# Moving the squares and the row statistics of the MLP norm into single slots of the tail's product loop

## The chip, the core and the metric

The kernel runs on one core of a Trainium2 chip. A core has a matrix engine (TensorE, PE in the profile, with its weight loads shown apart as PEld), a vector engine (VectorE, DVE), a scalar engine (ScalarE, ACT), GpSimd (POOL) and SyncE (SP), which here only issues DMAs. Matrix products are accumulated in PSUM, where eight banks of 128 x 512 float32 serve the stage in question; DVE and ACT read them out from there. The engines run side by side and wait for one another only through semaphores. The metric is the device time of one execution in microseconds (us), lower being better; the median over several runs is compared.

## The reference

A two-layer encoder trunk over 1024 positions and 1024 channels. Each layer is a mixer (layer 0: two recurrent head groups; layer 1: chunked attention), an output projection, an RMS-normed MLP with squared ReLU, and a gated embedding:

```python
x = x + mix
hf = rmsnorm(x, norm_ffn_g[i])
x = x + jnp.square(jax.nn.relu(hf @ mlp_w1[i])) @ mlp_w2[i]
x = x + rmsnorm(p[i] @ ple_w_proj[i], ple_norm_g[i]) * jax.nn.sigmoid(x @ ple_w_gate[i])
```

with `rmsnorm(x, g) = x * rsqrt(mean(x*x) + eps) * g`, the mean taken over the channels of one position. The change concerns only this mean for `hf`. ReLU and a positive factor for each position can be exchanged, so the kernel multiplies `x * g` by `w1` at once and brings in `rsqrt(...)`, squared, after the squared ReLU.

## The kernel before

Everything is held transposed: channels on the 128 partitions (eight tiles, `NK = 8`), positions along the free dimension (T = 1024, in two halves of `HB = 512`). Every float32 operand of a large product is split into a rounded part and a rest (`split`: one ACT copy, one DVE subtraction), and a product is three matrix instructions (`mm3`).

`tail(i, xsrc)` runs once for each layer, after the mixer. Its stages:

1. *Output projection.* For n = 0..7 the new residual is made: its first half lies in DRAM as `xh[n]`, the second half goes there as `xh2[n]` (tile name `xm`, line 1299).
2. *First MLP product*, in 16 units p = 0..15. A unit is a Strassen-like scheme of seven products m, run in `order = (1, 2, 5, 6, 7, 3, 4)`. One product is 12 matrix instructions into one bank of PSUM (`product`, line 1365). What follows it in the same iteration q of the inner loop is called its slot: sums and the squared ReLU on DVE and ACT (`plus`, `hidden`), and one of the seven weight pieces of the next unit (`prepare`). At a unit's start `raws(p + 1)` issues two 512 KB loads of weights on SP's queue into one of two tiles, `lt[2]` and `lt[3]`. For the first four units (`PLAIN = 4`) the hidden values are stored as they are; from the fifth on each is multiplied by `rs` (line 1384).
3. *Second MLP product*, then the *gate*.

The norm's statistics are made during stage 2. `squares(n)` (line 1309) loads the two halves of residual tile n (two DMAs of 256 KB on SP's queue, line 1314), squares them on ACT (line 1316, or 1319 for n = 0) and adds them on DVE into the two sums `accs` (line 1317). After unit p = 0, 1 and 2 come the squares 0 to 2, 3 to 5 and 6 to 7. Each takes a new tile with tag `pl`, of which there is one buffer, so that a square's loads wait for the addition of the square before. After unit 2 also come `row_stats` (line 366: eight products of the sums with a column of ones, fp32, which the trace shows as 16 matrix instructions, then 11 small DVE operations on 128 x 8 numbers for the inverse root, the result in `col`), `to_rows` (line 378: eight transposes with the identity, line 192, and two ACT copies out of PSUM) and one DVE product that squares `rs`.

Each engine executes its instructions in a fixed order. This order is made when the kernel is built, by a list scheduler that takes the program's order as priority and may put an instruction ahead of earlier ones that it reckons not to be ready; so loads, squares and weight pieces stand earlier in the trace than in the source. The fourth unit's products 5 and 6 stand ahead of the statistics in layer 0, but not in layer 1.

PSUM banks are taken in turn by `bank()` for products and statistics alike. `rs` is one tile of 128 x 1024 (tag `ph`), allocated before the loop and written by `to_rows` alone.

Of the kernel before, what the change touches and what calls it, by code (L numbers as in the profile page):

```python
# [8 lines left out]
F32 = mybir.dt.float32  # L9
# [3 lines left out]
ALU = mybir.AluOpType  # L13
# [4 lines left out]
P = 128  # L18
T = 1024
D = 1024  # L20
NK = D // P
HB = 512
# [87 lines left out]
class Trunk:  # L110
# [1091 lines left out]
    def tail(self, i, xsrc):  # L1202
# [9 lines left out]
        nc, tc, a = self.nc, self.tc, self.a  # L1212
        V, A, G = nc.vector, nc.scalar, nc.gpsimd
        last = i == 1
        hs = [slice(0, HB), slice(HB, T)]
        with ExitStack() as es:
# [16 lines left out]
            def ring(views):  # L1233
                state = [0]

                def f():
                    state[0] += 1
                    return views[(state[0] - 1) % len(views)]
                return f
            halves = lambda t: [t[:, q, :] for q in range(2)]  # L1240
            quarters = lambda t: [t[:, q, hs[e]] for q in range(2) for e in range(2)]
            two = lambda t: t.rearrange("p (q c) -> p q c", q=2)
            parts = lambda t: [two(v) for v in halves(t)]

            def tiles_x(dt):
                xw = [self.xp.tile([P, 3, T], dt, tag=f"xw{q}", name=f"xw{q}") for q in range(2)]
                return ([xw[k // 3][:, k % 3, :] for k in range(6)] +
                        [self.xp.tile([P, T], dt, tag=f"x{k}", name=f"x{k}") for k in (6, 7)])
# [11 lines left out]
            accs = [self.accp.tile([P, HB], F32, tag=f"acc{hf}", name="acc") for hf in range(2)]  # L1260
            col = self.cst.tile([P, NT], F32, tag="col", name="col")
# [4 lines left out]
            def split(c, s):  # L1266

                hi, lo = c[:, 0], c[:, 1]
                if len(s.shape) > 2:
                    hi, lo = (z.rearrange("p (j c) -> p j c", c=P) for z in (hi, lo))  # L1270
                A.copy(hi, s)  # L1271
                V.tensor_tensor(lo, s, hi.bitcast(F32), op=ALU.subtract)  # L1272
# [22 lines left out]
            def ev_out(n):  # L1295
# [10 lines left out]
                            split(cmb[m][j], u)  # L1306
                return f

            def squares(n):

                both = self.pre.tile([P, 2, HB], F32, tag="pl", name="xq")
                for hf, src in ((0, self.xh[n]), (1, self.xh2[n])):
                    t = both[:, hf]
                    nc.sync.dma_start(out=t, in_=src)
                    if n:
                        A.activation(t, t, AF.Square)
                        V.tensor_tensor(accs[hf], accs[hf], t, op=ALU.add)
                    else:
                        A.activation(accs[hf], t, AF.Square)
# [3 lines left out]
            def raws(p):  # L1323
                r = lt[3 - p % 2] if p else place(F32)
                for e in range(2):
                    nc.sync.dma_start(out=r[:, e], in_=a["w1"][i, 2 * p + e])
                prep[p] = [r[:, u].rearrange("p (j e c) -> p e j c", e=2, c=P)[:, v] for u in range(2) for v in range(2)], {}, []

            def prepare(p, m):

                (a11, a12, a21, a22), d, free = prep[p]
                if (p, m) == (0, 1):
                    d[m] = self.pre.tile([P, 2, HB], F32R, tag="pl", name="w1")
                else:
                    if not free:
                        free += parts(place(F32R))
                    d[m] = free.pop(0)
                if m == 5:

                    V.tensor_tensor(a21, a21, a22, op=ALU.add)  # L1340
                o, u, v = {1: (a11, None, None), 2: (a12, None, None), 5: (a21, None, None), 6: (a11, a21, a11),
                           4: (a22, None, None), 7: (a22, a22, a11), 3: (a12, a12, a11)}[m]
                if u is not None:
                    V.tensor_tensor(o, u, v, op=ALU.subtract)
                split(d[m], o)
# [14 lines left out]
            lt = lates([F32] * 4)  # L1360
            scr = ring([v for t in lt[0:2] for v in quarters(t)])
            rs = self.pre.tile([P, T], F32, tag="ph", name="rs")


            def product(p, m):
                ps, c = self.bank(), prep[p][1][m]
                for j in range(4):
                    o, z = slice(j * P, j * P + P), cmb[m][j]
                    self.mm3(ps, c[:, 0, o], c[:, 1, o], z[:, 0], z[:, 1], j == 0, j == 3)
                return ps  # L1370

            def plus(t, u, out=None):
                r = out if out is not None else scr()
                V.tensor_tensor(r, t, u, op=ALU.add)  # L1374
                return r

            def hidden(t, p, r, hf):

                A.activation(t, t, AF.Relu)  # L1379
                A.activation(t, t, AF.Square)  # L1380
                if p < PLAIN:
                    nc.scalar.dma_start(out=self.hd[2 * p + r][:, hs[hf]], in_=t)
                else:
                    V.tensor_tensor(t, t, rs[:, hs[hf]], op=ALU.mult)
                    if (r, hf) != (0, 1):
                        store(p, {(0, 0): 1, (1, 0): 2, (1, 1): 3}[r, hf], t)
                return t
# [4 lines left out]
            def differ(p, m, u, v, out=None):  # L1392
                t = out if out is not None else scr()
                V.tensor_tensor(t, u, v, op=ALU.subtract)
                store(p, m, t)
                return t
# [4 lines left out]
            def load_w2(g, u):  # L1401
                t, raw = place(F32R), self.pre.tile([P, 2, HB], F32, tag="pl", name="w2")
                for j in range(2):
                    nc.sync.dma_start(out=raw[:, j], in_=a["w2"][i, 2 * g + j, u])
                split(t, raw.rearrange("p j c -> p (j c)"))
                w2[g, u] = t[:, 0], t[:, 1]

            def fetch_hidden(g, k, t, raw):
                nc.sync.dma_start(out=raw, in_=self.hd[4 * g + k])
                return t, raw  # L1410

            def load_hidden(t, raw):
                V.tensor_tensor(raw, raw, rs, op=ALU.mult)
                split(t, raw)
# [32 lines left out]
                split(areas[m][q % 4], raw)  # L1447

            prep_order = (1, 2, 5, 6, 4, 7, 3)
            for m in prep_order[1:]:  # L1450
                prepare(0, m)
            for p in range(16):
                if p < 15:
                    raws(p + 1)
                else:
                    load_w2(0, 0)
                for q, m in enumerate(order):
                    ps = product(p, m)
                    if m == 1:
                        p1 = scr()  # L1460
                        A.copy(p1, ps)
                    elif m == 2:
                        c11 = hidden(plus(p1, ps), p, 0, 0)
                    elif m == 5:
                        p5 = ps
                    elif m == 6:
                        u2 = plus(p1, ps, p1)
                        u4 = plus(u2, p5)
                    elif m == 7:
                        u3 = plus(u2, ps, u2)  # L1470
                        c22 = hidden(plus(u3, p5), p, 1, 1)
                    elif m == 3:
                        c12 = hidden(plus(u4, ps, u4), p, 0, 1)
                        if p >= PLAIN:
                            differ(p, 7, c22, c12)
                            t1 = differ(p, 5, c12, c11, c12)
                            t2 = differ(p, 6, c22, t1)
                    else:
                        c21 = hidden(plus(u3, ps, u3), p, 1, 0)
                        if p >= PLAIN:  # L1480
                            differ(p, 4, c21, t2)
                    if p < 15:
                        prepare(p + 1, prep_order[q])
                    elif q == 1:
                        hid = [fetch_hidden(0, k, h0[k], lt[2 + k // 2][:, k % 2]) for k in range(4)]
                    elif 2 <= q < 6:
                        load_hidden(*hid[q - 2])
                    yield 0
                if p < 3:
                    for n in range(3 * p, min(3 * p + 3, NK)):  # L1490
                        squares(n)
                if p == 2:
                    self.row_stats(accs, col)
                    self.to_rows(col, rs)
                    V.tensor_tensor(rs, rs, rs, op=ALU.mult)
            x = tiles_x(F32)
            for k in range(NK):
                nc.sync.dma_start(out=x[k][:, hs[0]], in_=self.xh[k])
# [48 lines left out]
            for n in range(NB):  # L1547
                u, banks = n % 4, {}
                for s, m in enumerate(order2):
# [7 lines left out]
                    e, hf = goes[m]  # L1557
# [543 lines left out]
```

## Time and profile before

| what | value |
|---|---|
| median of 3 runs | 3112.31 us (3107.09 to 3116.35) |
| profiled execution | 3119.22 us, of which its span is 3117.5 us |
| mean granted clock of TensorE | 0.968 |
| layer 0, units of the first MLP product before the statistics | about 977 to 1042 us of the span |
| layer 1, the same | about 2388 to 2445 us of the span |
| statistics, layer 0 (first matrix instruction to the square of `rs`) | 1042.3 to 1051.6 us |
| statistics, layer 1 | 2445.1 to 2454.3 us |

The profile is taken from one execution. In its timeline a row is the start, the duration, the engine, the line, the operation, written tile `<-` read tiles, shapes and the number of instructions merged; in brackets the time for which the engine sat idle just before, and what ended that. Durations of matrix instructions overlap with their successors, so the pace of a run of them is read from the start of one row to the start of the next. In the windows view a row is a stretch: its length, then for PE, PEld, DVE, ACT and POOL the busy time and the count of instructions, then the granted clock of TensorE as a share of full speed, the busy share of the DMA engines and GB/s. In the view of waits a row tells who waited for whom: total, times, longest.

### The profile page before, as it was taken

Reading aid. Unit: us, or ns where it says so; the run is one execution under the profiler, and the core shown is the slowest. Engines: PE = TensorE matmul, PEld = TensorE weight load, DVE = VectorE, ACT = ScalarE, POOL = GpSimd, SP = SyncE. Lnnn points to the kernel's source line nnn. Section 1 sums busy time; section 2 is a strip of 40 time slices with the busy share of each in tenths; the row PEclk is TensorE's granted clock in tenths of the full one; section 3 lists DMA queues with packets and bytes.
Section 4 is the critical chain, followed back from the end, with each engine's and each line's share of the span. In section 5 each row is a group of like instructions: output and inputs, shape, how many; then the busy total and the mean of one; then the engine's idle time right before and its main releaser. Section 6 shows DMA issues by size and latency. Waiting matters only on the chain.

```text
span 3117.5 us, 47104 instructions
## 1 busy us (share of the span) xinstructions
PE 2998.6 (96%) x17288; PEld 2477.6 (79%) x17288; DVE 2222.7 (71%) x4518; ACT 1512.2 (49%) x2922; POOL 534.0 (17%) x978
## 2 busy tenths in 40 slices
PE   7999999999999999999999999999899999999999
PEld 5777777777777788888887988888788788888887
DVE  6646675667758788877866676776768688888862
ACT  4323433344436544544433577777766545444431
POOL 6524442443510000000005111110210000000002
PEclk8989999999999999999999999999999999999999
DMA  4212112212356444754424111110256444754433
GB/s 137 71 42 72 44 58 72 63 51 70 103 168 206 148 156 150 259 168 153 126 98 136 52 33 33 42 46 16 71 176 215 147 152 149 246 179 147 135 108 102
DMA packets 187639, 358.45 MB, mean 115 GB/s; under 512 B 45712, under 2 KB 47888, under 8 KB 187408
## 3 DMA queue, kind: packets, MB, share of 16 engines
q1 hardware_dynamic: 158608, 303.00, 30.0%
q10 hardware_dynamic: 28800, 52.44, 4.4%
q8 instruction: 136, 2.23, 0.3%
q14 instruction: 95, 0.78, 0.1%
HBM read 262.04 MB, written 93.32 MB: 114 GB/s over the span
## 4 chain that ended last, share of the span: by engine, by line
PE 81%; DVE 9%; ACT 4%; DMA 3%; issue 1%; POOL 1%; SPq 0%; DVEq 0%; POOLq 0%; ACTq 0%
PE dps L177 68%; PE ch L177 2%; PE po L177 2%; PE iz L177 1%; PE pm L177 1%; PE tp L177 1%; PE pt L192 1%; DVE ptile L350 1%; PE py L177 1%; PE sn L177 1%; DVE pb L1941 1%; ACT pb L1954 1%; PE pp L177 1%; DMA wraw<-in_w_out 1%; PE st L177 1%
## 5 line engine op out<-in xcount | busy, mean ns | idle before, releaser
L177 PE MATMUL dps<-r,act 128*128 128x512 f32 x3528 | 831.5, 393 | 0.0
L177 PEld LDWEIGHTS dps<-r,act 128*128 128x128 f32 x3528 | 664.8, 189 | 146.7
L177 PE MATMUL dps<-xg,whi 128*128 128x512 f32 x1280 | 439.7, 424 | 12.7 <-ACT xg L352 7.4
L1598 POOL TENSOR_TENSOR pn<-pn,prs 128x512 f32<-128x512 f32 x32 | 45.0, 1409 | 1577.1 <-ACT prs L386 1480.0
L177 PE MATMUL dps<-wq,act 128*128 128x384 f32 x1536 | 306.4, 345 | 6.9 <-DVE vs L1850 3.1
L177 PEld LDWEIGHTS dps<-xg,whi 128*128 128x128 f32 x1280 | 237.2, 198 | 64.8 <-ACT xg L352 7.4
L177 PEld LDWEIGHTS dps<-wq,act 128*128 128x128 f32 x1536 | 266.7, 191 | 11.1 <-DVE vs L1850 5.3
L177 PE MATMUL dps<-xg,wlo 128*128 128x512 f32 x640 | 260.1, 407 | 1.3 <-DVE wlo L304 1.3
L177 PE MATMUL dps<-late,act 128*128 128x512 f32 x960 | 229.2, 392 | 0.0
L177 PEld LDWEIGHTS dps<-late,act 128*128 128x128 f32 x960 | 180.3, 188 | 39.7
L1271 ACT CAST act<-act 128x512 fp32r<-128x512 f32 (+1 forms) x223 | 137.6, 649 | 129.3 <-PE dps L177 60.7
L1374 DVE TENSOR_TENSOR late<-late,dps 128x512 f32<-128x512 f32 x224 | 152.3, 684 | 62.5 <-PE dps L177 54.2
L1271 ACT CAST act<-late 128x512 fp32r<-128x512 f32 x210 | 124.1, 618 | 136.3 <-PE dps L177 91.1
L177 PE MATMUL dps<-act 128*128 128x512 f32 x672 | 165.5, 393 | 0.1
L1272 DVE TENSOR_TENSOR act<-act 128x512 fp32r<-128x512 f32 (+1 forms) x223 | 154.5, 719 | 4.2 <-ACT act L1271 4.2
L177 PEld LDWEIGHTS dps<-xg,wlo 128*128 128x128 f32 x640 | 125.9, 197 | 32.1 <-issue 2.3
L177 PEld LDWEIGHTS dps<-act 128*128 128x128 f32 x672 | 126.1, 188 | 29.2 <-DVE xw L1506 0.5
L1272 DVE TENSOR_TENSOR act<-late,act 128x512 fp32r<-128x512 f32 x210 | 141.4, 687 | 10.9 <-ACT act L1271 9.0
L303 ACT CAST whi<-wraw 128x1024 fp32r<-128x1024 f32 x78 | 81.9, 1050 | 122.4 <-PE dps L177 83.2
L1506 DVE TENSOR_TENSOR xw<-xw,dps 128x512 f32<-128x512 f32 x174 | 117.7, 681 | 29.6 <-PE dps L177 29.6
L177 PE MATMUL dps<-xw,act 128*128 128x512 f32 x576 | 138.4, 391 | 0.0
L1379 ACT ACTIVATE late<-late 128x512 f32<-128x512 f32 x128 | 80.2, 629 | 117.1 <-DVE late L1374 106.8
(482 smaller groups left out, 5652.0 us busy)
## 6 DMA issues: line engine op xcount, KB each, us to landing
hb<-late ACTq DMA_DIRECT2D x168, 256.0 KB
act<-hb SPq DMA_DIRECT2D x138, 256.0 KB
late<-in_w SPq DMA_DIRECT2D x60, 512.0 KB
wraw<-in_w_in SPq DMA_DIRECT2D x56, 512.0 KB
act<-in_w SPq DMA_DIRECT2D x96, 256.0 KB
braw<-hb SPq DMA_DIRECT2D x72, 256.0 KB
wraw<-in_w_out SPq DMA_DIRECT2D x21, 512.0 KB
wraw<-in_w_qkv SPq DMA_DIRECT2D x21, 512.0 KB
```

The lines of the kernel that those rows point to most:

```text
L177: return self.begin(self.nc.tensor.matmul(out, lhsT, rhs, start=start, stop=stop, skip_group_check=again))
L192: return self.begin(self.nc.tensor.transpose(out, in_, ident))
L303: nc.scalar.copy(hi, raw)
L350: nc.vector.tensor_tensor(dst[:, 1, sl], src, dst[:, 0, sl].bitcast(F32), op=ALU.subtract)
L1271: A.copy(hi, s)
L1272: V.tensor_tensor(lo, s, hi.bitcast(F32), op=ALU.subtract)
L1374: V.tensor_tensor(r, t, u, op=ALU.add)
L1379: A.activation(t, t, AF.Relu)
L1506: V.tensor_tensor(x[n][:, hs[hf]], x[n][:, hs[hf]], ps, op=ALU.add)
L1598: G.tensor_tensor(pn, pn, prs[:, sl], op=ALU.mult)
L1941: V.tensor_tensor_reduce(S, pn[:, 0:nn * P], toep[:, (3 - nn) * P:], op0=ALU.add, op1=ALU.max, scale=1.0, scalar=NEG, accum_out=mx[:, 0:1])
L1954: A.activation(S, S, AF.Exp, bias=mx[:, 2:3], accum_out=l[:, 0:1])
```

## The change

The squares' loads become a function of their own, `fetch_squares(n)`. Square 0 is staged in `rs` itself (seen as two halves), square 1 in the `pl` tile, and square n from then on in the tile of square n - 2. The load of square 0 is issued before the loop over the units, that of 1 and 2 right after square 0, and that of n + 2 right after square n.

The squares stand in single slots, given by a list of pairs (unit p, iteration q); eight pairs for n = 0..7. `row_stats` stands in slot (3, 0), after the first product of the fourth unit, `to_rows` and the square of `rs` in slot (3, 3), after its fourth product. The numbers of instructions and of DMAs on each engine and their sizes remain the same.

```diff
+            def fetch_squares(n):
+                if n == 0:
+                    t = two(rs)
+                else:
+                    t = sq[n - 2] if n > 1 else self.pre.tile([P, 2, HB], F32, tag="pl", name="xq")
+                for hf, src in ((0, self.xh[n]), (1, self.xh2[n])):
+                    nc.sync.dma_start(out=t[:, hf], in_=src)
+                sq[n] = t
+
             def squares(n):
-                both = self.pre.tile([P, 2, HB], F32, tag="pl", name="xq")
-                for hf, src in ((0, self.xh[n]), (1, self.xh2[n])):
-                    t = both[:, hf]
-                    nc.sync.dma_start(out=t, in_=src)
+                for hf in range(2):
+                    t = sq[n][:, hf]
                     if n:
                         A.activation(t, t, AF.Square)
                         V.tensor_tensor(accs[hf], accs[hf], t, op=ALU.add)
...
             rs = self.pre.tile([P, T], F32, tag="ph", name="rs")
+            sq = {}
+            fetch_squares(0)
...
             prep_order = (1, 2, 5, 6, 4, 7, 3)
+            sums = [(0, 1), (0, 3), (0, 6), (1, 1), (1, 4), (1, 6), (2, 2), (2, 4)]
...
                         load_hidden(*hid[q - 2])
+                    if (p, q) in sums:
+                        n = sums.index((p, q))
+                        squares(n)
+                        if n == 0:
+                            fetch_squares(1)
+                        if n + 2 < NK:
+                            fetch_squares(n + 2)
+                    elif (p, q) == (3, 0):
+                        self.row_stats(accs, col)
+                    elif (p, q) == (3, 3):
+                        self.to_rows(col, rs)
+                        V.tensor_tensor(rs, rs, rs, op=ALU.mult)
                     yield 0
-                if p < 3:
-                    for n in range(3 * p, min(3 * p + 3, NK)):
-                        squares(n)
-                if p == 2:
-                    self.row_stats(accs, col)
-                    self.to_rows(col, rs)
-                    V.tensor_tensor(rs, rs, rs, op=ALU.mult)
```

## The prediction

> **What bounds the kernel now.** I read the page first, then the waits of PE over the tail, then PE's timeline around the statistics, and last the clock in windows.
>
> ```profile
> span 3117.5 us, 47104 instructions
> PE 2998.6 (96%) x17288; PEld 2477.6 (79%) x17288; DVE 2222.7 (71%) x4518; ACT 1512.2 (49%) x2922; POOL 534.0 (17%) x978
> ```
>
> PE is busy in 96% of the span, so an edit is worth what it takes out of PE's idle or slowed time. The waits of PE between 980 and 1700 us, which hold layer 0's whole MLP, are two rows:
>
> ```profile
> PE dps L177 <- DVE acc L1317: 2.8, 1, 2.8
> PE dps L192 <- DVE col L291: 2.3, 1, 2.3
> ```
>
> Both belong to the statistics: the ones products wait for the last addition of squares, the transposes for the inverse root. PE's timeline there, layer 0 and then layer 1:
>
> ```profile
> 1033.91 4.24 PE L177 MATMUL dps<-xw,act 128*128 128x512 f32 x18
> 1037.99 1.52 PE L177 MATMUL dps<-x,act 128*128 128x512 f32 x6
> 1042.26 3.20 PE L177 MATMUL dps<-ones,acc 128*128 128x1 f32 x16 [2.75 <-DVE acc L1317]
> 1047.73 1.97 PE L192 MATMUL dps<-ident,col 128*128 128x128 f32 x8 [2.27 <-DVE col L291]
> 1049.35 12.90 PE L177 MATMUL dps<-r,act 128*128 128x512 f32 x48
> 1062.09 2.93 PE L177 MATMUL dps<-act 128*128 128x512 f32 x12
> 1064.86 5.67 PE L177 MATMUL dps<-r,act 128*128 128x512 f32 x24
> 1070.37 4.29 PE L177 MATMUL dps<-xw,act 128*128 128x512 f32 x18
> ...
> 2439.39 2.93 PE L177 MATMUL dps<-act 128*128 128x512 f32 x12
> 2445.06 3.13 PE L177 MATMUL dps<-ones,acc 128*128 128x1 f32 x16 [2.74 <-DVE acc L1317]
> 2450.47 1.97 PE L192 MATMUL dps<-ident,col 128*128 128x128 f32 x8 [2.27 <-DVE col L291]
> 2452.09 7.49 PE L177 MATMUL dps<-r,act 128*128 128x512 f32 x24
> 2459.41 2.91 PE L177 MATMUL dps<-xw,act 128*128 128x512 f32 x12
> ```
>
> The undisturbed pace is 24 matrix instructions from 1064.86 to 1070.37, 5.51 us or 0.2296 us each; a product (12) is 2.76 us. After both statistics the pace is worse. The clock in windows tells why (the third column from the right is PE's granted clock):
>
> ```profile
> 1039.50:1042.26 2.76, 0.01 (x1) 0.00 (x0) 1.44 (x3) 1.37 (x3) 0.00 (x0) 1.00 0.74 269
> 1045.50:1047.70 2.20, 0.00 (x0) 0.00 (x0) 1.83 (x11) 0.00 (x0) 0.00 (x0) 0.50 0.92 323
> 1049.35:1053.00 3.65, 3.65 (x11) 2.88 (x10) 1.55 (x2) 0.70 (x2) 0.00 (x0) 0.51 0.00 0
> 1053.00:1057.00 4.00, 4.00 (x19) 3.30 (x18) 0.15 (x1) 0.79 (x2) 0.00 (x0) 1.00 0.01 4
> ```
>
> The clock is still full in the first idle stretch, half in the second, and stays at half for the first 3.65 us of the products that follow. So a layer pays for the statistics in waits, in a half clock while they run, and in a half clock behind them.
>
> What they cost in all. **Layer 0:** the six instructions from 1037.99 end their turn at 1037.99 + 6 x 0.2296 = 1039.37, the next product starts at 1049.35: 9.98 us. The 48 that follow take 1062.09 - 1049.35 = 12.74 us in place of 11.02: 1.72 us. Together 11.70. **Layer 1:** 2439.39 + 2.76 = 2442.15 to 2452.09 is 9.94 us, and 24 in 7.32 us in place of 5.51 is 1.81: 11.75. Both layers: 23.45 us.
>
> Whatever PE gets back there reaches the end, because up to the next stages PE has no idle time in which it could be lost:
>
> ```profile
> 1049.35:1620.00 570.65, 570.54 (x2486) 466.93 (x2485) 456.39 (x705) 257.35 (x424) 3.01 (x2) 1.00 0.46 155
> 2452.10:3110.00 657.90, 657.90 (x2869) 538.91 (x2868) 485.83 (x743) 271.75 (x445) 21.73 (x16) 1.00 0.44 149
> ```
>
> **The change part by part.** No instruction goes away, so the statistics' own work on PE remains, and its price must be found at full clock. The same operations in places where PE was kept busy (and the ones products once more at half clock), in the timeline and the windows:
>
> ```profile
> 854.12 1.05 PE L177 MATMUL dps<-ones,xg 128*128 128x1 f32 x8
> 855.10 0.92 PE L177 MATMUL pm<-AR,b 64*128 64x128 f32 x4
> ...
> 1615.52 1.03 PE L192 MATMUL dps<-ident,prsc 128*128 128x128 f32 x8
> 1616.31 5.99 PE L177 MATMUL dps<-r,act 128*128 128x512 f32 x25
> ...
> 854.12:855.10 0.98, 0.98 (x10) 0.96 (x8) 0.98 (x3) 0.59 (x2) 0.90 (x2) 1.00 1.08 410
> 2275.34:2277.07 1.73, 1.73 (x9) 1.73 (x9) 1.40 (x3) 0.81 (x2) 1.08 (x1) 0.50 0.81 225
> ```
>
> Eight ones instructions take 0.98 us at clock 1.00 (1.73 at 0.50), eight transposes 1616.31 - 1615.52 = 0.79. For 16 and 8 that is 1.96 + 0.79 = 2.75 us for each layer, 5.5 for both. The dear end is today's half-clock price, 3.20 for the ones and 1049.35 - 1047.73 = 1.62 for the transposes, 4.82 a layer. I take 2.75, because in the new place both groups stand between products at the undisturbed pace, as at 854 and 1615 us.
>
> *The transposes' wait (2.27 us).* `row_stats` now stands after the fourth unit's first product, `to_rows` after its fourth. Three products, 3 x 2.76 = 8.3 us, lie between, and the inverse root's eleven DVE operations took 2.2 us (window 1045.50 to 1047.70). The cover is over three times what it must hide. If it went, 2.27 would be back. What is behind the small operations on DVE are read-outs of PSUM, which have eight banks of room. `rs` is first used a unit later.
>
> *The ones' wait (2.75 us).* Here something has to come earlier: the last addition. Squares today run in a single tile:
>
> ```profile
> 992.50 0.33 SPq L1314 DMA_DIRECT2D xq<-xh  x1
> ...
> 1037.67 0.32 SPq L1314 DMA_DIRECT2D xq<-xh  x1
> ...
> 1042.79 0.69 DVE L1317 TENSOR_TENSOR acc<-acc,xq 128x512 f32<-128x512 f32 x1
> ...
> SPq L1314 <- DVE acc L1317: 25.2, 6, 6.3
> ```
>
> Eight loads lie between 992.50 and 1037.67, 45.17 / 7 = 6.45 us apart; SP waited 25.2 us for additions in between. The chain of load, square, addition in one tile is what made the sums late, until 1043.5. With two tiles two such chains run beside each other; even if each keeps 6.45 us, the last of four in the second tile is loaded at 992.5 + 3 x 6.45 = 1011.9 and added some 6 us later, by 1018. The other bound is that nothing stands earlier than its slot. Square 7's is after the third unit's fifth product. In layer 0 the third unit ends at 1033.91 (the rows at 1033.91 and 1037.99 are products 5 and 6 of the fourth, put ahead), its fifth product two products earlier, at 1028.4; with the additions of that slot about 1032. The ones now come after one more product, 1033.91 + 2.76 = 1036.7. In layer 1 the third unit ends at 2442.15, and the same reckoning gives 2436.6 for the slot, 2440 for the sums, 2444.9 for the ones. Between 4 and 5 us of room at the late bound, so I set this wait to 0; if the cover is gone, see the second rival.
>
> *The half clock* behind the statistics (1.72 and 1.81 us) then has no idle time ahead of it; I set it to 0.
>
> The Trainium skill, "TensorE: Matmul & The Clock Gate", section "Part 1: The HAM clock gate", says that the array falls to half clock after at least one idle window of about 3.4 us and returns after about 3.4 us of work. By that rule a wait of 2.75 us alone would not have halved the clock here, and the trace differs: half clock came with 2.75 us of wait and one-column products behind it, which hints that these hardly count as work. The return agrees, 3.65 us. By the rule, a group of 1.96 us between full products can't fill a window, and the sum stands; if one-column products with a little idle time were enough, it would be the third rival.
>
> *Moved loads, squares, additions.* Per layer 16 DMAs on SP, 16 squares on ACT, 14 additions on DVE, as before but earlier:
>
> ```profile
> L1316 ACT ACTIVATE xq<-xq x28: 613/631/636, 999.6 to 2444.7; 128x512 f32<-128x512 f32 x28
> L1317 DVE TENSOR_TENSOR acc<-acc,xq x28: 678/686/693, 1000.3 to 2445.5; 128x512 f32<-128x512 f32 x28
> 2409.00:2428.00 19.00, 19.00 (x85) 15.56 (x84) 18.98 (x33) 14.86 (x28) 0.00 (x0) 1.00 0.65 217
> 1025.83 1.41 DVE L1374 TENSOR_TENSOR late<-late,dps 128x512 f32<-128x512 f32 x2 [0.28 <-PE dps L177]
> ```
>
> DVE is full in the second unit (18.98 of 19.00 us), and additions that come forward push read-outs and weight pieces back there. Were they all added to the early units, 14 x 0.686 = 9.6 us of DVE a layer; nothing, if they fall into gaps. In 2409 to 2428 PE was busy all the time beside the full DVE, and at 1025.83 DVE had to wait for PE, so it was level with PE; a delay must eat the free banks first, each 2.76 us of PE's time. I take 0. `raws` stands behind the new loads on SP, which wait for additions; it fetches a unit ahead, so I take 0 there too.
>
> **Sum.** 23.45 - 5.5 = 17.95 us less: the profiled execution's 3119.22 (span 3117.5 and 1.7 around it) becomes 3101.3. That execution lies 6.9 above the median of the runs, and I take the same difference off the median: 3112.31 - 17.95 = 3094.4.
>
> **The rivals.**
>
> *Second: the sums are still late.* If ACT and DVE reach the squares no earlier than before, only the transposes' wait goes. A layer then keeps 2.75 of wait, 3.20 of half-clock ones, about 1.76 of slowed products, and 0.79 of transposes: 8.50 in place of about 11.72, 6.5 us less in all: 3105.8. For it: the order is made by a scheduler whose reckoning erred by these very waits. Against: SP's 25.2 us of waits, which the second tile takes away, and the late bound above.
>
> *Third: each group halves the clock by itself.* 3.20 + 1.62 + 2 x 1.76 = 8.34 a layer, 6.8 us less: 3105.5. Against it stands the clock of 1.00 at 854.
>
> *Fourth, slower: the early units choke.* Place: DVE and ACT in the first two units of both layers. If all 14 additions and 16 squares came onto PE's path, 9.6 + 16 x 0.631 = 19.7 us, with 1.76 of half clock behind it 21.5 a layer, against 8.97 gained: 25 us slower, 3137. It decides from a stall of PE of 8.97 us a layer. For it: 18.98 of 19.00. Against: PE's unbroken work beside that, and the free banks.
>
> *Fifth, slower: the rest is put in another order.* The order of all that follows is made anew. Layer 1's mixer is where PE has idle time that can grow:
>
> ```profile
> 1700.00:2040.00 340.00, 310.17 (x1920) 293.66 (x1919) 233.74 (x738) 230.05 (x537) 49.84 (x52) 0.96 0.14 47
> 2040.00:2392.00 352.00, 330.55 (x1875) 292.80 (x1876) 252.66 (x698) 247.56 (x541) 38.91 (x35) 0.98 0.30 100
> ```
>
> 29.8 + 21.5 = 51.3 us idle; half as much again is 25.6, which gives 3120. It outweighs the gain from 17.95 on. Against: the two layers differ in their order (two products ahead in one) and lost the same 2.75 and 2.27.
>
> **How the numbers follow.** A measurement of this kernel tells about 0.3% (9.3 us) from no change: faster is below 3103.0, slower above 3121.6. Forecast 0.74; sums late 0.09; clock 0.05; choked units 0.05; another order 0.07, of which 0.02 stay within 0.3%. So faster 0.74, same 0.09 + 0.05 + 0.02 = 0.16, slower 0.10. The forecast's own range: from 2.75 to 4.82 us for a layer's statistics the gain is 17.95 to 13.8, 3094 to 3099, and with the scatter of the runs before (5.2 below and 4.0 above the median) 3089 to 3103. The range for all reaches over the second and third rival with that scatter, and by a few us below for an order that happens to be better: 3086 to 3111.
>
> **What would show it.** In the changed kernel's PE timeline: one product between the third unit and the ones products, three between these and the transposes, no bracket on either, about 1.96 and 0.79 us, clock 1.00 through the fourth unit. The squares' loads two ahead of their use, the last addition before 1033 and 2441. A bracket on the ones shows the second rival; no bracket and a clock of 0.5 the third; new waits of PE in the first three units the fourth; more idle time of PE between 1700 and 2392 the fifth. The forecast is wrong if the fourth unit is clean and the total does not fall by at least 13 us.

## The result and the profile after

The changed kernel takes 3100.53 us (median of 20 runs, 3089.67 to 3113.56) against 3113.9 us for the kernel before (20 runs): a ratio of 0.9952, 95% interval 0.9937 to 0.9967, so 10 to 20 us less; the medians differ by 13.4 us. The forecast was 17.95 us less, to 3094.4 us.

The runs of one kernel scatter by over 20 us, and the gain in question is smaller. The trace is sharper, because PE passes fixed marks: the output projection's products (`xg,act`), the last large group of the gate (`r,late`) in layer 0, and the output projection (`act,late`) in layer 1. Their rows in the view of the product banks, first for the kernel before, then for the changed one (count, least, median and greatest duration in ns, then the start of the first and of the last):

```profile
L177 PE MATMUL dps<-r,late x288: 388/389/395, 1638.4 to 1703.5; 128*128 128x512 f32 x144
L177 PE MATMUL dps<-act,late x144: 393/394/398, 2350.7 to 2385.7; 128*128 128x512 f32 x144
L177 PE MATMUL dps<-xg,act x120: 388/392/397, 948.5 to 977.1; 128*128 128x512 f32 x120
```

```profile
L177 PE MATMUL dps<-r,late x288: 388/389/395, 1627.4 to 1692.5; 128*128 128x512 f32 x144
L177 PE MATMUL dps<-act,late x144: 392/394/399, 2341.4 to 2376.4; 128*128 128x512 f32 x144
L177 PE MATMUL dps<-xg,act x120: 388/392/397, 946.9 to 975.5; 128*128 128x512 f32 x120
```

Four stretches follow: up to the start of `xg,act` (layer 0's mixer), from there to `r,late` (tail 0), on to `act,late` (rest of layer 0 and layer 1's mixer), and on to the end of the span (tail 1). Before, tail 0 is 1638.4 - 948.5 = 689.9 us and tail 1 is 3117.5 - 2350.7 = 766.8. After, 680.5 and, with the span of 3099.3, 757.9. The tails, which hold all that was edited, lost 9.4 + 8.9 = 18.3 us; the other two stretches moved by -1.6 and +1.7.

PE's timeline in the changed kernel around the statistics, layer 0, then layer 1:

```profile
1032.32 2.93 PE L177 MATMUL dps<-r,act 128*128 128x512 f32 x12
1035.09 1.84 PE L177 MATMUL dps<-ones,acc 128*128 128x1 f32 x16
1036.79 3.01 PE L177 MATMUL dps<-r,act 128*128 128x512 f32 x12
1039.63 4.29 PE L177 MATMUL dps<-xw,act 128*128 128x512 f32 x18
1043.76 1.52 PE L177 MATMUL dps<-x,act 128*128 128x512 f32 x6
1045.12 1.56 PE L177 MATMUL dps<-r,act 128*128 128x512 f32 x6
1046.52 1.04 PE L192 MATMUL dps<-ident,col 128*128 128x128 f32 x8
1047.31 4.36 PE L177 MATMUL dps<-r,act 128*128 128x512 f32 x18
...
2435.81 1.84 PE L177 MATMUL dps<-ones,acc 128*128 128x1 f32 x16
2437.51 3.01 PE L177 MATMUL dps<-r,act 128*128 128x512 f32 x12
...
2445.85 1.03 PE L192 MATMUL dps<-ident,col 128*128 128x128 f32 x8
2446.64 5.75 PE L177 MATMUL dps<-r,act 128*128 128x512 f32 x24
```

No row has a bracket: PE waits nowhere around the statistics. The ones products stand behind one product of the fourth unit, the transposes behind three more (three and a half in layer 0). From start to start the ones take 1.70 us and the transposes 0.79. The windows of the changed kernel show the clock (third column from the right) at full speed on both groups and between them in layer 0; in layer 1 it is 1.00 on both groups too:

```profile
1035.09:1036.79 1.70, 1.70 (x17) 1.70 (x16) 1.70 (x4) 1.31 (x3) 0.00 (x0) 1.00 0.40 154
1036.79:1040.00 3.21, 3.21 (x16) 2.66 (x16) 1.95 (x11) 1.43 (x3) 0.00 (x0) 1.00 0.42 163
1046.52:1047.31 0.79, 0.79 (x9) 0.79 (x8) 0.79 (x3) 0.15 (x1) 0.00 (x0) 1.00 0.15 36
```

The sums were complete early, as DVE's and SP's rows of the changed kernel tell (its lines are shifted: 1316 issues a square's load, 1325 adds):

```profile
1014.50 0.32 SPq L1316 DMA_DIRECT2D xq<-xm  x1
...
1022.78 0.68 DVE L1325 TENSOR_TENSOR acc<-acc,xq 128x512 f32<-128x512 f32 x1
...
2416.53 0.67 DVE L1325 TENSOR_TENSOR acc<-acc,xq 128x512 f32<-128x512 f32 x1
```

The last load of a square left at 1014.5 in place of 1038, the last addition ended at 1023.5 in place of 1043.5. The ones came at 1035.1: 11.6 us of room in layer 0, and in layer 1, by the same rows, 18.6.

### The profile page after: what moved, and what is told of

Read it like the earlier page. It is cut to its first block, busy times and chain, and to the rows that moved or that the text cites. A ratio compares the mean times of both kernels' runs of the same rounds, so it can differ in the third digit from the quotient of the medians.

```text
span 3099.3 us, 47124 instructions
## 1 busy us (share of the span) xinstructions
PE 2991.6 (97%) x17288; PEld 2473.5 (80%) x17288; DVE 2222.2 (72%) x4518; ACT 1509.8 (49%) x2922; POOL 533.8 (17%) x978
## 4 chain that ended last, share of the span: by engine, by line
PE 82%; DVE 9%; ACT 3%; DMA 2%; issue 2%; POOL 1%; DVEq 0%; SPq 0%; POOLq 0%; ACTq 0%
PE dps L177 69%; PE ch L177 2%; PE po L177 2%; PE iz L177 1%; PE pm L177 1%; PE pt L192 1%; PE tp L177 1%; DVE ptile L350 1%; PE sn L177 1%; PE py L177 1%; DVE pb L1957 1%; PE pp L177 1%; ACT pb L1970 1%; DVE f L1057 1%; DMA wraw<-in_w_qkv 1%
## 5 line engine op out<-in xcount | busy, mean ns | idle before, releaser
L177 PEld LDWEIGHTS dps<-act 128*128 128x128 f32 x672 | 126.2, 188 | 28.6
```

What stands on the lines that cost most here:

```text
L177: return self.begin(self.nc.tensor.matmul(out, lhsT, rhs, start=start, stop=stop, skip_group_check=again))
```

## Experiments

All experiments are compared by the two tails as worked out above, each read from one profiled execution. Two kernels were run twice; their tails agree to 0.3 us each time. The medians come from three batches, in which the kernel before had 3113.9, 3111.31 and 3113.39 us (the first two rows; the next four; the last four), so they are to be compared only within a batch.

| kernel | tail 0 | tail 1 | median us (runs) |
|---|---|---|---|
| before | 689.9 | 766.8 | 3113.9 (20) |
| the change | 680.5 | 757.9 | 3100.53 (20) |
| place alone | 690.0 | 757.8 | 3101.56 (11) |
| tiles alone | 681.9 | 765.2 | 3105.28 (12) |
| later place, one tile | 680.4 | 757.8 | 3093.03 (6) |
| squares on DVE | 683.7 | 764.2 | 3097.67 (1) |
| the change again | 680.7 | 757.9 | 3091.97 (7) |
| later place again | 680.7 | 757.8 | 3098.71 (9) |
| one product between | 681.6 | 757.9 | 3089.81 (1) |
| squares on DVE, later transposes | 683.5 | 758.7 | 3092.19 (1) |

A part of the differences in tail 0 arises ahead of the MLP. In five of the ten executions (place alone, tiles alone, both with the squares on DVE, one product between) PE waits once more in the output projection, for a weight piece. In place alone, where nothing ahead of the fourth unit was edited, PE's row and a row of ACT some ten us earlier are:

```profile
955.61 11.28 PE L177 MATMUL dps<-xg,act 128*128 128x512 f32 x48 [0.75 <-DVE act L1272]
...
944.89 1.05 ACT L1271 CAST act<-act 128x1024 fp32r<-128x1024 f32 x1 [2.27 <-DMA act<-in_w_out]
```

ACT waits there for a load of the projection's weights, DVE for ACT, and from then on DVE works without a pause up to the piece that PE waits for. ACT's wait is 2.2 to 2.8 us in these five executions, 0.9 to 1.7 us in the other five, in which PE does not wait. From the first to the last start of `xg,act` it is 29.4 to 30.0 us in the five and 28.6 to 28.8 in the others, so that 0.8 to 1.4 us of their tail 0 come from this load. Whether its delay is chance or goes with the kernel is not shown.

### Place alone

The kernel before, with only the statistics moved:

```diff
+                    if (p, q) == (3, 0):
+                        self.row_stats(accs, col)
+                    elif (p, q) == (3, 3):
+                        self.to_rows(col, rs)
+                        V.tensor_tensor(rs, rs, rs, op=ALU.mult)
                     yield 0
                 if p < 3:
                     for n in range(3 * p, min(3 * p + 3, NK)):
                         squares(n)
-                if p == 2:
-                    self.row_stats(accs, col)
-                    self.to_rows(col, rs)
-                    V.tensor_tensor(rs, rs, rs, op=ALU.mult)
```

> Only the statistics' place is changed: squares in one tile after units 0 to 2 as before, row_stats in slot (3, 0), to_rows in slot (3, 3). In its order PE has one product ahead of the first four ones products in layer 0. Theory (two waits of their own: the ones wait for late sums, the transposes for want of products in between): the transposes' wait is gone in both layers; the sums are no earlier than in the kernel before (about 70 us after the layer's output projection), so PE still waits for them, by 1 to 6 us in layer 0, where the ones come about 5 us earlier than before, and 0 to 2 us in layer 1. Gain 10 to 15 us of the 18. Rival A (the place does it all): no wait of PE left, 18 us. Rival B (the second tile does it all, the place is idle): both waits stay, within 2 us of the kernel before.

Layer 1 gained the whole 9 us, layer 0 nothing. PE's timeline in this kernel, layer 0 and layer 1, and the windows with the clock in layer 0:

```profile
1037.90 1.87 PE L177 MATMUL dps<-ones,acc 128*128 128x1 f32 x8 [5.27 <-DVE acc L1317]
1039.63 5.02 PE L177 MATMUL dps<-r,act 128*128 128x512 f32 x12
1044.49 0.39 PE L177 MATMUL dps<-xw,act 128*128 128x512 f32 x1
...
2433.69 5.67 PE L177 MATMUL dps<-r,act 128*128 128x512 f32 x24
2439.20 1.32 PE L177 MATMUL dps<-xw,act 128*128 128x512 f32 x5
2440.36 1.84 PE L177 MATMUL dps<-ones,acc 128*128 128x1 f32 x16
...
1037.90:1039.63 1.73, 1.73 (x8) 1.73 (x9) 0.69 (x1) 0.50 (x1) 0.00 (x0) 0.50 0.00 0
1039.63:1044.49 4.86, 4.86 (x13) 3.83 (x14) 0.00 (x0) 0.00 (x0) 0.00 (x0) 0.55 0.36 108
```

The sums come no earlier, and in layer 0 the ones were due behind a single product of the fourth unit, where two stand in the kernel before, so PE waited 5.27 us in place of 2.75. The clock was at half behind the wait: the product behind the first ones takes 1044.49 - 1039.63 = 4.86 us in place of 2.76. With the half-clock ones (half of them in 1.73 us in place of 0.85) that is 5.27 + 2.10 + 0.88 = 8.25 us above the change, of the 9.5 us by which tail 0 is longer; the late load in the output projection makes 1.1 us of the rest. In layer 1 the order put two products and five instructions of a third ahead of the ones (2433.69 and 2439.20), and there was no wait. Both rivals fall: the place does not do it all, nor is it idle.

### Tiles alone

The change, with the statistics put back behind the third unit:

```diff
-                    elif (p, q) == (3, 0):
-                        self.row_stats(accs, col)
-                    elif (p, q) == (3, 3):
-                        self.to_rows(col, rs)
-                        V.tensor_tensor(rs, rs, rs, op=ALU.mult)
                     yield 0
+                if p == 2:
+                    self.row_stats(accs, col)
+                    self.to_rows(col, rs)
+                    V.tensor_tensor(rs, rs, rs, op=ALU.mult)
```

> Only the squares are changed: two tiles, loads two ahead, in the slots of the change; the statistics stand after the third unit as before. Theory: the sums are complete some 10 us before the ones are due, so no wait for the last addition in either layer. The transposes follow the ones with nothing between them in the source; where the order puts products of the fourth unit between, nothing is lost and the layer's gain is the full 9 us; where it puts none, 2.3 us of wait stay, with up to 1.8 us of half clock behind, and the gain is 5 to 7 us. Together 10 to 18 us. Rival A (the place does it all): the waits of before stay, under 2 us of gain.

As expected no wait for the sums was left in either layer, and layer 0, in whose order two products stand between ones and transposes, kept 8.0 us of gain; with the late load in the output projection (1.4 us) set aside it is 9.4, the whole. In layer 1 nothing stands between, and there the expectation (5 to 7 us) was too mild: 1.6 us of gain, 9.6 in all. PE's and DVE's rows of this kernel, layer 1:

```profile
2432.51 1.84 PE L177 MATMUL dps<-ones,acc 128*128 128x1 f32 x16
2439.83 1.97 PE L192 MATMUL dps<-ident,col 128*128 128x128 f32 x8 [5.47 <-DVE col L291]
...
2435.32 0.69 DVE L1348 TENSOR_TENSOR late<-late 128x512 f32<-128x512 f32 x1 [0.72 <-DMA late<-in_w]
...
2436.53 0.16 DVE L375 TENSOR_SCALAR ms<-dps 128x8 f32<-128x8 f32 x1
2436.61 0.68 DVE L1352 TENSOR_TENSOR late<-late 128x512 f32<-128x512 f32 x1
2437.21 0.68 DVE L1272 TENSOR_TENSOR act<-late,act 128x512 fp32r<-128x512 f32 x1
2437.81 0.16 DVE L286 TENSOR_SCALAR col<-ms 128x8 int32<-128x8 int32 x1
```

The ones were done by 2434.3; the inverse root began at 2436.53 and was interrupted. DVE keeps its order, and weight pieces of a later unit stood ahead of the eleven small operations, one of them waiting for its own load. The clock fell to half during the wait, and the window of the transposes shows it:

```profile
2439.83:2441.45 1.62, 1.62 (x8) 1.62 (x9) 0.00 (x0) 0.47 (x1) 0.00 (x0) 0.50 0.04 10
```

Against the change, layer 1 pays 5.47 us of wait, 0.83 for transposes at half clock (1.62 in place of 0.79) and 1.09 for slowed products behind (24 in 6.60 us in place of 5.51): 7.39, where tail 1 is 7.3 longer. The cover that the transposes need is therefore not the 2.2 us of the inverse root but this plus DVE's queue, here 5.5 us.

### Later place, one tile

The kernel before, with the statistics three products later than in the change, and neither a second tile nor slots for the squares:

```diff
+                    if (p, q) == (3, 3):
+                        self.row_stats(accs, col)
+                    elif (p, q) == (3, 6):
+                        self.to_rows(col, rs)
+                        V.tensor_tensor(rs, rs, rs, op=ALU.mult)
                     yield 0
                 if p < 3:
                     for n in range(3 * p, min(3 * p + 3, NK)):
                         squares(n)
-                if p == 2:
-                    self.row_stats(accs, col)
-                    self.to_rows(col, rs)
-                    V.tensor_tensor(rs, rs, rs, op=ALU.mult)
```

> Squares in one tile after units 0 to 2 as before; row_stats in slot (3, 3), to_rows in slot (3, 6), three products later than in the change. Theory: the sums, late as before, are complete some 5 us before the ones are due, three products lie between ones and transposes; no wait of PE, full clock, rs is there before the fifth unit's first hidden values need it. The whole gain of 18 us without the second tile. Rival B (the second tile is needed): waits stay and the gain is under 10 us. Rival (rs comes too late): DVE waits for rs in the fifth unit, and PE behind it.

The tails equal the change's to 0.1 us. PE's timeline of this kernel, layer 0:

```profile
1032.76 1.84 PE L177 MATMUL dps<-ones,acc 128*128 128x1 f32 x16
1034.46 4.61 PE L177 MATMUL dps<-r,act 128*128 128x512 f32 x19
1038.91 2.91 PE L177 MATMUL dps<-act 128*128 128x512 f32 x12
1041.66 1.52 PE L177 MATMUL dps<-xw,act 128*128 128x512 f32 x6
1043.02 1.04 PE L192 MATMUL dps<-ident,col 128*128 128x128 f32 x8
1043.81 5.75 PE L177 MATMUL dps<-r,act 128*128 128x512 f32 x24
```

No bracket, full pace. The sums are as late as before: the last addition ends 95.4 us after the tail's mark (95.0 in the kernel before, 76.6 in the change), 2.2 us ahead of the ones. Nothing needs `rs` before the fifth unit (line 1384 reads it first at 1051.7), so a place behind the late sums does as well as earlier sums. The median was lower than the change's, and the trace's mixer was shorter: it ended at 935.2 us. Whether that belongs to the kernel was asked of two repeats on one chip.

> The changed kernel once more, beside the next one on the same chip, to see how much of a difference between two kernels is the scatter of the parts that no edit touches (layer 0's mixer ended at 947 to 948 us of the span in the kernels before and after, at 935 in the kernel with the later place). Theory: the two tails take 680.5 and 757.9 us as before, within 1 us, and the mixer's end moves by up to 15 us from one execution to another. Rival (the mixer's time belongs to the kernel): it ends at 947 again.

> The kernel with one tile and the later place (slots (3, 3) and (3, 6)) once more. Theory: its tails equal those of the change, and so do its runs, within their interval; the 7 us by which its median was lower came from the mixer's scatter. Rival: it is faster than the change by some 7 us again, on the same chip.

Now the change had the lower median (3091.97, ratio to the kernel before 0.9934, 0.9911 to 0.9958; the later place 3098.71, ratio 0.9949, 0.9932 to 0.9966). Both intervals hold the other's ratio. The tails are the same again. The 7 us in favour of the later place did not come back in the medians. In the traces, however, the mixer ended at 945.4 in the change and 938.6 in the later place, each within 3.5 us of its first execution; the 15 us of movement that were expected were not seen. So two traces of each kernel don't exclude that a few us of the mixer's time go with the kernel; that they do is not shown either, as the medians turned round.

### Squares on DVE

The change, with the squares of n = 1..7 taken from ACT to DVE:

```diff
                     if n:
-                        A.activation(t, t, AF.Square)
+                        V.tensor_tensor(t, t, t, op=ALU.mult)
                         V.tensor_tensor(accs[hf], accs[hf], t, op=ALU.add)
```

> The change with the 14 squares of n = 1..7 made by DVE in place of ACT: 14 more DVE operations of about 0.68 us, 9.5 us a layer, in the stretch where DVE is fullest. Theory (DVE has room because PE has free banks and weight pieces made a unit ahead): no new wait of PE in the first three units, the time within 3 us of the changed kernel. Rival (the early units choke once DVE is full): PE waits for read-outs or weight pieces, 5 us and more a layer.

The theory expected 3 us at most and missed: the tails lost 3.2 and 6.3 us against the change (0.9 of the 3.2 is the late load in the output projection). DVE's rows of this kernel, layer 1, and PE's wait:

```profile
2432.16 0.16 DVE L375 TENSOR_SCALAR ms<-dps 128x8 f32<-128x8 f32 x1
...
2441.00 0.69 DVE L1348 TENSOR_TENSOR late<-late 128x512 f32<-128x512 f32 x1 [1.82 <-DMA late<-in_w]
2441.61 0.16 DVE L291 SCALAR_TENSOR_TENSOR col<-rsw,col 128x8 f32<-128x8 f32 x1
...
2442.21 0.17 DVE L291 SCALAR_TENSOR_TENSOR col<-rsw,col 128x8 f32<-128x8 f32 x1
...
2442.52 1.94 PE L192 MATMUL dps<-ident,col 128*128 128x128 f32 x8 [3.16 <-DVE col L291]
```

Eleven operations of 2.2 us are stretched over 10.2 us, from 2432.16 to 2442.38, because other work stands between them, in the end a weight piece that waits 1.82 us for its load. To see whether that was all, this kernel was given its transposes later (the edit against this kernel):

```diff
-                    elif (p, q) == (3, 3):
+                    elif (p, q) == (3, 6):
                         self.to_rows(col, rs)
```

> The squares on DVE again, as in e6, with to_rows in slot (3, 6) in place of (3, 3). In e6 layer 1's tail lost 6.3 us to a wait of 3.2 us for the inverse root and the half clock behind it, layer 0's 3.2 us to waits of 1.1 and 0.6 us. Theory (a fuller DVE costs only because the inverse root is late; the products themselves have room): layer 1's wait is gone and its tail is within 1 us of the change's 757.9; layer 0's small waits may stay. Rival (a full DVE chokes PE whatever the place): both tails stay 3 us and more above the change's.

Layer 1 came within 0.8 us of the change, so nearly all of the loss there was the late inverse root and its half clock; what is left is one wait of 0.55 us for a weight piece in the second unit. Layer 0 kept 3.0 us, with two small waits that show the other rival at work in a small way (PE's rows of this kernel):

```profile
1001.45 8.95 PE L177 MATMUL dps<-r,act 128*128 128x512 f32 x38 [1.04 <-DVE late L1384]
1010.98 2.57 PE L177 MATMUL dps<-r,act 128*128 128x512 f32 x10 [0.58 <-DVE act L1272]
```

These are a late read-out of PSUM and a late weight piece, in the second and third unit. From start to start they cost 1.2 and 0.8 us, 2.0 together; the late load in the output projection adds 0.8. So with 14 more operations DVE is over the edge by some 2 us in layer 0 and by 0.7 in layer 1. This rests on one execution of each of the two kernels; the two waits of layer 0 stand in both.

### One product between

The change, with the transposes and the square of `rs` two products earlier:

```diff
-                    elif (p, q) == (3, 3):
+                    elif (p, q) == (3, 1):
                         self.to_rows(col, rs)
                         V.tensor_tensor(rs, rs, rs, op=ALU.mult)
```

> The change with to_rows and the square of rs in slot (3, 1): one product, 2.8 us, in the source between the ones products and the transposes in place of three; the order made has three there in layer 0 (products 5 and 6 put ahead) and may have one in layer 1. Theory: the inverse root needs 2.2 us of DVE plus what stands before it in DVE's order (in the change it ended 3 to 5 us after the ones); with one product between, PE waits 0 to 3 us in that layer, and none in the other. Rival (2.8 us of cover is enough for 2.2 us of work): no wait, tails as in the change.

No wait in layer 1 either, and tail 1 as in the change: the rival holds here. DVE's and PE's rows of this kernel show by how little:

```profile
2426.44 0.17 DVE L375 TENSOR_SCALAR ms<-dps 128x8 f32<-128x8 f32 x1 [0.98 <-PE dps L177]
...
2428.46 0.17 DVE L291 SCALAR_TENSOR_TENSOR col<-rsw,col 128x8 f32<-128x8 f32 x1
...
2429.11 1.04 PE L192 MATMUL dps<-ident,col 128*128 128x128 f32 x8
```

DVE happened to be waiting for the ones, ran its eleven operations in one piece, and was done 0.48 us before the transposes. Tail 0 is 1.1 us longer than in the change, which is the late load in the output projection (29.7 us for `xg,act` in place of 28.6).

## Why the prediction was right

- **The bound.** PE set the end, and time won in the tails reached it: 18.3 us in the tails against 17.95 forecast. The median fell by 13.4 us in the first comparison and by 21.4 in the second (3113.39 to 3091.97). That the first lies 6 us above the forecast of 3094.4 and still in its range says little, with runs of one kernel over 20 us apart; it is the tails that bear the mechanism out.
- **The cost before, 23.45 us,** was read rightly as waits, half-clock work and half-clock products. The place-alone kernel shows all three parts once more, in layer 0 alone: 5.27 us of wait, the clock at 0.50, a product in 4.86 us.
- **The price of what stays** was slightly too high: 1.70 us for the ones in place of 1.96, 0.79 for the transposes as forecast. Together 2.49 a layer in place of 2.75. With it the sum would be 23.45 - 4.98 = 18.47, where the tails lost 18.3.
- **The wait for the inverse root** went, but the reckoning "over three times what it must hide" took the 2.2 us of the small operations alone. In the changed kernel's layer 0 they ran from 1037.32 to 1042.07, 4.8 us, with other work between. "If it went, 2.27 would be back" was too mild: without the cover in the tiles-alone kernel's layer 1, 5.47 us and a half clock came.
- **The wait for the sums** went, with far more room than the late bound allowed: the last addition ended at 1023.5, between the early bound of 1018 and the late one of 1032. But "something has to come earlier" was wrong as a statement on what is needed: with the later place the sums stayed late, and the gain was the same.
- **The second rival** (late sums, 6.5 us of gain) was built in the place-alone kernel. There the gain is 9.0 us, all of it in layer 1: the rival's per-layer sum didn't allow that the same late sums cost one layer nothing and the other 5.27 us.
- **The third rival** (each group halves the clock by itself) did not occur: the clock was 1.00 on both groups. The hint that one-column products hardly count as work is not needed for the half clock before: in another kernel it fell after 2.0 us of idle time with full products ahead of it (last section).
- **The fourth rival** (choked early units) did not occur, and 14 more DVE operations a layer show that it was near: some 2 us of waits in layer 0.
- **The fifth** (another order) did not occur: the stretch from `r,late` to `act,late` took 712.3 us before and 714.0 after.

## What to carry to other kernels

A small chain from PE to a vector engine and back (sums, inverse root, transposes) costs three things when it stands in PE's order without other products: the wait, its own work at half clock, and half clock behind it. Put products between its two ends, and count the cover against the chain plus what stands ahead of it in the vector engine's order, not against the chain alone. Ask first how late the result may come: a later place can be worth as much as faster inputs. And where the runs scatter by more than the gain, measure between fixed marks of the trace.

## What the runs showed of the hardware

- The clock was at half behind PE's waits of 2.75 us (kernel before), 3.16 us (squares on DVE, layer 1), 5.27 and 5.47 us (place alone, tiles alone). It stayed full behind a wait of 1.12 us (squares on DVE, layer 0) and on 1.70 us of one-column products between full ones (the change). Where it turned differs. With the squares on DVE full products ran up to 2439.36, and the clock was full for 2.0 us of the wait only:

```profile
2439.36:2441.40 2.04, 0.00 (x0) 0.00 (x0) 0.40 (x1) 0.00 (x0) 0.00 (x0) 1.00 0.97 321
2441.40:2442.52 1.12, 0.00 (x1) 0.03 (x1) 0.87 (x5) 0.00 (x0) 0.00 (x0) 0.52 0.94 338
```

  In place alone it turned after 4.5 us of the wait, in tiles alone after 2.5 us (behind 1.8 us of one-column products), in the kernel before 0.4 to 0.5 us after the wait's end. It was back at full 2.2 to 4.4 us after the next full products began. So no single length of idle time fits all; what else decides was not tried. The Trainium skill, "TensorE: Matmul & The Clock Gate", section "Part 1: The HAM clock gate", asks for an idle window of about 3.4 us. The idle time of 2.0 us is shorter, with full products right ahead of it, so the trace differs.
- Layer 0's mixer, which no edit touches, ended at 946.9 and 945.4 us in two executions of the change, at 935.2 and 938.6 in two of the later place and at 936.1 with one product between, while the tails of the first four agree to 0.3 us. So in these executions the totals differ mainly by what comes before the tail; the cause was not sought.
